# Three unused SBUF tiles that move the start addresses of two operand rings in a two-layer decoder trunk

## The chip, the cores and the metric

The kernel runs on one core of one Trainium2 chip. The metric is the device time of one execution in microseconds, the median of the runs shown; lower is better. Engines are named as the profile names them: PE (TensorE's matmuls), PEld (TensorE's weight loads), DVE (VectorE), ACT (ScalarE), POOL (GpSimd), SP (the queue that issues all DMAs here).

## What is computed

Two layers over 256 tokens of 1,024 channels, all in float32. Cut to the parts that matter here:

```python
def hybrid_layer(x, ...):
    h = rms_norm(x, g_mix)
    z = h @ w_in                       # 1024 -> 6072 columns
    ...                                # z is split among three mixers and their gates
    o_a = mla_mixer(...); o_b = conv_mixer(...); o_c = nsa_mixer(...)
    x = x + (g_a * o_a + g_b * o_b + g_c * o_c) @ w_out
    h = rms_norm(x, g_ffn)
    x = x + jnp.square(jax.nn.relu(h @ w_ff1)) @ w_ff2    # 1024 -> 4096 -> 1024
    return x
```

## The kernel before

**Every large product is three products.** A float32 operand is split into a high part (`hi`, rounded to the PE's `float32r` format by ACT, line 153 for weights) and a low part (`lo`, the remainder, by DVE, line 154). PE then adds up high by high, high by low and low by high. Weights are streamed from DRAM in pieces of 128 x 1,024 numbers by `raw` (line 138, a ring of five buffers) and split by `piece` into one of two rings: ring one is four `hi` and four `lo` buffers of the pool `wp`; ring two is the tag `big` of the pool `ap`, five buffers of 8 KB, where a tile holds two pieces side by side (`hi2`, `lo2`).

**Which operand is stationary.** In `gemm_b` (lines 163 to 165) the weight slice, 128 x 128, is the stationary operand, which a weight load brings into the array, and the activations, 256 tokens wide, are the moving one. So run the products into `psB` (the input projection's columns for convolution, low ranks and gates), the three mixer projections `wo` of 256 columns, and the first feed-forward product `ff1` (the profile cuts the name to `ff`). In `gemm_a` (lines 171 to 173) it is the other way round: 128 tokens of the activations are stationary and up to 512 weight columns move. So run `psA` (three groups of the input projection), the output projection (also called `wo` in the profile, at lines 171 to 173), and the second feed-forward product into `f0` to `f3` (`f` in the profile), whose stationary tiles are `rh` and `rl`, the two parts of the squared ReLU (lines 890 and 892).

**Activation rings.** The tag `hh` of the pool `ap` holds two buffers for the high parts, `hl` two for the low parts. Their tenants are in turn `hh`/`hl` (normed input), `oh`/`ol` (attention outputs), `mh`/`ml` (gated sum, in the first buffer), `h2`/`l2` (second norm's input). The convolution's output `yh` lies in the ring `cv` and `yl` in the ring `s2`, both of the pool `sp`. `rh` and `rl` lie in the ring `pa` of the pool `sp`, six buffers of 2 KB.

**Order.** Inside the mixer part of a layer a table (`TRACE`, with the priorities of `URGENCY`) sets the order; the framework's scheduler then places every instruction on its engine's queue. The feed-forward part is a loop over 16 groups (line 903): `ff1(gi + 1)` issues 48 matmuls of 256 columns, then `acc_pass` issues 24 matmuls of 512 columns for group `gi` (two weight pieces, two token blocks, two column halves, three products each). In the last three groups the order differs (`tail`), and there the pieces of the last group lie in ring one.

**Addresses.** Pools lie one behind the other in a partition and tags in order of first request; a tile's start is rounded up to 32 bytes. Every slice that the products below read begins a multiple of 512 bytes into its tile (only the 312-column pieces of the first `psA` group differ), so the start of the tile modulo 512 is also that of the slice. For a matmul's moving slice and stationary slice, "320 apart" means below that these two remainders differ by 320.

| tiles | first byte of the ring, before | modulo 512 | modulo 64 |
|---|---|---|---|
| `hi`, `lo` (ring one) | 54,912 / 71,296 | 128 | 0 |
| `hh`, `oh`, `mh`, `h2` | 87,680 | 128 | 0 |
| `hl`, `ol`, `ml`, `l2` | 104,064 | 128 | 0 |
| `hi2`, `lo2` (ring two, `big`) | 137,664 | 448 | 0 |
| `yl` (`s2`) | 182,912 | 128 | 0 |
| `yh`, `ca`, `upad` (`cv`), two buffers | 195,552 and 200,128 | 480 and 448 | 32 and 0 |
| `rh`, `rl`, softmax tiles `nP`, `mP`, ... (`pa`) | 209,824 | 416 | 32 |

`yh` is in the buffer at 480 in the first layer and at 448 in the second; the tap accumulator `ca` is in the other one.

Of the kernel before, what the change touches and what calls it, by code (L numbers as in the profile page):

```python
# [8 lines left out]
F32 = mybir.dt.float32  # L9
# [7 lines left out]
P = 128  # L17
# [68 lines left out]
def trunk_kernel(ctx: ExitStack, tc: tile.TileContext, A, out, depth=DEPTH):  # L86
# [4 lines left out]
    ap_ = ctx.enter_context(tc.tile_pool(name="ap", bufs=1))  # L91
    sp = ctx.enter_context(tc.tile_pool(name="sp", bufs=2))
# [5 lines left out]
    def stat(n, name, dt=F32):  # L98
        return sp.tile([P, n], dt, tag="st%d" % n, name=name, bufs=2 if n > 64 else 6)
# [36 lines left out]
    def raw(src, n):  # L136
        r = wp.tile([P, 1024], F32, tag="raw", name="raw", bufs=RB)[:, :n]
        nc.sync.dma_start(out=r, in_=src)
        return r
# [27 lines left out]
    def gemm_a(ps, ah, al, wh, wl, ks, first=True, last=True):  # L167

        n = len(ks)
        for i, (kw, ka) in enumerate(ks):  # L170
            mm(ps, lhsT=ah(ka), rhs=wh(kw), start=(first and i == 0), stop=False)  # L171
            mm(ps, lhsT=ah(ka), rhs=wl(kw), start=False, stop=False)  # L172
            mm(ps, lhsT=al(ka), rhs=wh(kw), start=False, stop=(last and i == n - 1))  # L173
# [5 lines left out]
    def rsqrt(v, p, n, name):  # L179

        s = stat(n, name + "_s", I32)
        y = stat(n, name + "_y")
        h = stat(n, name + "_h")
        t = stat(n, name + "_t")
        s, y, h, t = s[:p], y[:p], h[:p], t[:p]
        ts(out=s, in0=v.bitcast(I32), scalar1=1, scalar2=None, op0=ALU.logical_shift_right)
        ts(out=h, in0=v, scalar1=-0.5, scalar2=None, op0=ALU.mult)
        ts(out=y.bitcast(I32), in0=s, scalar1=-1, scalar2=0x5f3759df, op0=ALU.mult, op1=ALU.add)
        for _ in range(3):
            if n == 1:  # L190
                ts(out=t, in0=y, scalar1=y, scalar2=h, op0=ALU.mult, op1=ALU.mult)
                ts(out=y, in0=t, scalar1=1.5, scalar2=y, op0=ALU.add, op1=ALU.mult)
            else:
                tt(out=t, in0=y, in1=y, op=ALU.mult)
                tt(out=t, in0=t, in1=h, op=ALU.mult)
                stt(out=y, in0=t, scalar=1.5, in1=y, op0=ALU.add, op1=ALU.mult)
        return y
# [56 lines left out]
    def layer(l):  # L254
# [18 lines left out]
        def pa(name, dt=F32):  # L273
            return sp.tile([P, 512], dt, tag="pa", bufs=PA, name=name)
# [3 lines left out]
        col = lambda ap: ap.rearrange("p (n o) -> p n o", o=1)  # L278


        hh = ap_.tile([P, 8, T], R32, tag="hh", name="hh", bufs=2)
        hl = ap_.tile([P, 8, T], R32, tag="hl", name="hl", bufs=2)
        grow = raw(bass.AP(tensor=A["gmix"].tensor, offset=A["gmix"].offset + l * D, ap=[[0, P], [1, D]]), D)
        vs = stat(2, "n1v")
# [36 lines left out]
        def part_a(i):  # L321

            return ([psum(t, "psA%d" % i) for t in (("at", "at"), ("po", "ch"), ("at", "at"))[i]],
                    [piece(A["wA%d" % i][l, kp], 2, ring=int(i == 1), half=kp % 2) for kp in range(4)])

        def add_a(i, pw, b, kps=range(4)):
            for kp in kps:
                wh, wl = pw[1][kp]
                gemm_a(pw[0][b][:, :A_COLS[i]], hA(hh, b), hA(hl, b), lambda k: wh[:, k, :], lambda k: wl[:, k, :],
                       [(k, kp * 2 + k) for k in range(2)], first=(kp == 0), last=(kp == 3))  # L330
# [59 lines left out]
        def a_queries():  # L390
            nonlocal nr
            pw = part_a(2)
            psA = pw[0]
            for kp in range(4):
                for b in range(NB):
                    add_a(2, pw, b, (kp,))
            for b in range(NB):
                pq = psA[b].rearrange("p (g j d) -> p g j d", g=2, j=4)
                sq = pa("nsqq").rearrange("p (n d) -> p n d", d=DH)
                qn.append(pa("qn").rearrange("p (n d) -> p n d", d=DH))  # L400
                act(sq.rearrange("p (j g) d -> p g j d", g=2), pq, AF.Square)
                act(qn[b].rearrange("p (j g) d -> p g j d", g=2), pq, AF.Copy)
                nc.vector.tensor_reduce(out=nst[:, b, 0:8], in_=sq, axis=AX.X, op=ALU.add)
            nv = stat(24, "nv")
            ts(out=nv, in0=nst.rearrange("p b n -> p (b n)"), scalar1=1.0 / DH, scalar2=EPS, op0=ALU.mult, op1=ALU.add)
            nr = rsqrt(nv, P, 24, "nr").rearrange("p (b n) -> p b n", b=NB)
# [412 lines left out]
        def gated(m, c2):  # L819
# [13 lines left out]
            if len(done[c2]) == 3:  # L833
                if mh is None:
# [5 lines left out]
        oh = ap_.tile([P, 8, T], R32, tag="hh", name="oh", bufs=2)  # L840
        ol = ap_.tile([P, 8, T], R32, tag="hl", name="ol", bufs=2)
        steps = {"a": a_products, "a0": a_compressed, "a1": a_keys, "a2": a_queries, "qk": nsa_qk, "glu": glu, "lr": low_rank, "lrn": low_rank_norm, "ckv": compress_kv, "csc": compress_scores,
                 "nsa": lambda j: nsa_attention(j, (oh, ol)), "mla": lambda j: mla_attention(j, (oh, ol)),
                 "rk": rotary_keys, "mq": mla_q, "mk": mla_k, "tap": lambda i: taps(TAPS[i], TAPS[i + 1]), "cn": conv_norm,
# [80 lines left out]
    for l in range(depth):  # L925
        layer(l)
# [129 lines left out]
```

## Time and profile before

| | |
|---|---|
| median of 3 runs | 930.91 us (928.43, 930.91, 931.38) |
| the profiled execution's own time | 932.83 us |
| its span, first to last instruction | 930.9 us |
| granted clock, mean over the span | 0.996 of full speed |

The profiled execution took 1.92 us longer than the median of the runs and 1.9 us longer than its own span. A row of the profile gives an instruction's start and a modelled end. A matmul's listed duration holds its pipeline's latency, so the time that a matmul costs in a stream is not its duration but the distance from its start to the next start; the text below calls this the pitch, and takes it from two starts and the number of matmuls between them.

### The profile page before, as it was taken

What the parts mean: (1) busy time and instruction counts of PE and PEld (TensorE: products, weight loads), DVE (VectorE), ACT (ScalarE), POOL (GpSimd) and SP (SyncE); (2) the same over time, 40 slices, a digit from 0 to 9 for tenths busy, and PEclk for the clock granted to TensorE, in tenths of its full rate; (3) what the DMA queues carried; (4) which work ended last, traced back from release to release, by engine and by line L of the source; (5) the groups of instructions that cost most, each with busy time, mean ns of one, the idle gap of its engine ahead of it and who ended that gap; (6) DMA issues with size and microseconds to landing.
All of it is one profiled execution on the core that took longest, in us unless ns stands there. A gap on an engine that the chain in (4) does not pass through costs nothing.

```text
span 930.9 us, 16102 instructions
## 1 busy us (share of the span) xinstructions
PE 909.1 (98%) x6214; PEld 805.4 (87%) x6214; DVE 642.6 (69%) x1431; ACT 538.4 (58%) x987; POOL 27.2 (3%) x80
## 2 busy tenths in 40 slices
PE   5999999999999999999999999999999999999998
PEld 4899888689988999999878989877999789999996
DVE  6598889775787655555576989979558775555552
ACT  5456566897367644444355575679865565444430
POOL 3210000000000000000001000000000000000000
PEclk9999899999999999999999999999999999999999
DMA  8654522334565655555345553225435476555521
GB/s 292 209 166 151 203 87 80 99 126 140 182 204 194 223 194 182 190 190 186 101 158 187 162 215 106 74 80 181 159 101 194 150 259 203 185 187 186 189 91 46
DMA packets 43133, 151.55 MB, mean 163 GB/s; under 512 B 4784, under 2 KB 5680, under 8 KB 43056
## 3 DMA queue, kind: packets, MB, share of 16 engines
q1 hardware_dynamic: 43056, 150.52, 49.3%
q8 instruction: 49, 0.80, 0.3%
q14 instruction: 28, 0.23, 0.1%
HBM read 149.45 MB, written 1.05 MB: 162 GB/s over the span
## 4 chain that ended last, share of the span: by engine, by line
PE 86%; DVE 6%; DMA 4%; ACT 2%; issue 1%; SPq 0%; DVEq 0%; ACTq 0%
PE psB L163 7%; PE psB L165 7%; PE psB L164 7%; PE f L173 6%; PE f L171 6%; PE f L172 6%; PE ff L164 6%; PE ff L163 6%; PE ff L165 6%; DVE lo L154 3%; PE wo L164 2%; PE wo L163 2%; PE wo L165 2%; PE nS L576 2%; PE uq L638 2%; PE psA L172 2%
## 5 line engine op out<-in xcount | busy, mean ns | idle before, releaser
L154 DVE TENSOR_TENSOR lo<-raw,hi 128x1024 fp32r<-128x1024 f32 (+1 forms) x266 | 317.6, 1209 | 173.4 <-ACT hi L153 135.2
L153 ACT ACTIVATE hi<-raw 128x1024 fp32r<-128x1024 f32 (+1 forms) x266 | 274.7, 1048 | 262.0 <-DMA raw<-in_ff_dram 102.3
L163 PE MATMUL psB<-hh,hi 128*128 128x256 f32 x592 | 173.3, 293 | 1.4 <-ACT ug L749 1.4
L165 PE MATMUL psB<-hh,lo 128*128 128x256 f32 x592 | 171.2, 291 | 0.0
L164 PE MATMUL psB<-hl,hi 128*128 128x256 f32 x592 | 170.4, 288 | 0.0
L165 PE MATMUL ff<-h,lo 128*128 128x256 f32 x512 | 144.5, 283 | 0.0
L163 PE MATMUL ff<-h,hi 128*128 128x256 f32 x512 | 144.4, 283 | 0.0
L164 PE MATMUL ff<-l,hi 128*128 128x256 f32 x512 | 144.3, 283 | 0.0
L163 PEld LDWEIGHTS psB<-hh,hi 128*128 128x128 f32 x592 | 113.9, 192 | 8.2 <-issue 4.4
L165 PEld LDWEIGHTS psB<-hh,lo 128*128 128x128 f32 x592 | 113.7, 193 | 3.0 <-issue 2.6
L164 PEld LDWEIGHTS psB<-hl,hi 128*128 128x128 f32 x592 | 114.0, 193 | 0.3
L758 DVE SCALAR_TENSOR_TENSOR ca<-upad,cols,ca 128x256 f32<-128x256 f32 x240 | 103.6, 477 | 0.3
L173 PE MATMUL f<-hi,rl 128*128 128x512 f32 x256 | 101.2, 395 | 1.4 <-DVE rl L892 0.7
L171 PE MATMUL f<-hi,rh 128*128 128x512 f32 x256 | 101.2, 395 | 0.0
L172 PE MATMUL f<-lo,rh 128*128 128x512 f32 x256 | 101.0, 395 | 0.0
L163 PEld LDWEIGHTS ff<-h,hi 128*128 128x128 f32 x512 | 97.9, 192 | 1.2
L164 PEld LDWEIGHTS ff<-l,hi 128*128 128x128 f32 x512 | 98.0, 192 | 1.1
L165 PEld LDWEIGHTS ff<-h,lo 128*128 128x128 f32 x512 | 98.0, 192 | 0.0
L173 PEld LDWEIGHTS f<-hi,rl 128*128 128x128 f32 x256 | 48.0, 188 | 13.8 <-DVE rl L892 2.5
L171 PEld LDWEIGHTS f<-hi,rh 128*128 128x128 f32 x256 | 48.1, 188 | 10.4 <-ACT rh L890 0.2
L172 PEld LDWEIGHTS f<-lo,rh 128*128 128x128 f32 x256 | 48.0, 188 | 10.3
L172 PE MATMUL psA<-lo,hh 128*128 128x512 f32 (+1 forms) x96 | 36.0, 375 | 2.1 <-DVE lo L154 2.1
(279 smaller groups left out, 1422.5 us busy)
## 6 DMA issues: line engine op xcount, KB each, us to landing
raw<-in_ff_dram SPq DMA_DIRECT2D x128, 512.0 KB, 4.1
raw<-in_wB_dram SPq DMA_DIRECT2D x74, 512.0 KB, 3.8
raw<-in_wA_dram SPq DMA_DIRECT2D x16, 512.0 KB, 4.4
raw<-in_w_out_dram SPq DMA_DIRECT2D x16, 512.0 KB, 3.5
raw<-in_wo_nsa_dram SPq DMA_DIRECT2D x8, 512.0 KB, 4.7
raw<-in_wo_mla_dram SPq DMA_DIRECT2D x8, 512.0 KB, 4.0
raw<-in_wconv_dram SPq DMA_DIRECT2D x8, 512.0 KB, 3.9
raw<-in_wA_dram SPq DMA_DIRECT2D x8, 312.0 KB, 5.2
```

The lines of the kernel that those rows point to most:

```text
L153: act(hi, r, AF.Copy)
L154: tt(out=lo, in0=r, in1=hi.bitcast(F32), op=ALU.subtract)
L163: mm(ps, lhsT=wh(kw), rhs=ah(ka), start=(first and i == 0), stop=False)
L164: mm(ps, lhsT=wh(kw), rhs=al(ka), start=False, stop=False)
L165: mm(ps, lhsT=wl(kw), rhs=ah(ka), start=False, stop=(last and i == n - 1))
L171: mm(ps, lhsT=ah(ka), rhs=wh(kw), start=(first and i == 0), stop=False)
L172: mm(ps, lhsT=ah(ka), rhs=wl(kw), start=False, stop=False)
L173: mm(ps, lhsT=al(ka), rhs=wh(kw), start=False, stop=(last and i == n - 1))
L576: mm(pS[g].rearrange("p (h z k) -> p h z k", h=nj, z=2)[:, i], lhsT=qTn[gs, 2 * jp + j, b * P:(b + 1) * P], rhs=kTn[gs, :, 0:nk], start=Tr ...
L638: mm(ps[:, :n], lhsT=cq[:, k, b * P:(b + 1) * P], rhs=w[i][:, c0:c0 + n], start=(i == 0), stop=(i == len(ks) - 1))
L758: stt(out=ca[:, i], in0=upad[:, i, k:k + T], scalar=K("wdw", 31 * i + k), in1=ca[:, i], op0=ALU.mult, op1=ALU.add)
```

## The change

Three tiles are requested that nothing writes or reads: 80 floats (320 bytes of each partition) ahead of the ring `hh`, 48 floats (192 bytes) ahead of `hl`, and 8 floats (32 bytes) in `sp`, at the point where the ring `pa` is first requested.

```diff
@@ layer(l), line 280 on
+        if l == 0:
+            ap_.tile([P, 80], F32, tag="gap0", name="gap0")
         hh = ap_.tile([P, 8, T], R32, tag="hh", name="hh", bufs=2)
+        if l == 0:
+            ap_.tile([P, 48], F32, tag="gap1", name="gap1")
         hl = ap_.tile([P, 8, T], R32, tag="hl", name="hl", bufs=2)
@@ a_queries()
                     add_a(2, pw, b, (kp,))
+            if l == 0:
+                sp.tile([P, 8], F32, tag="gap2", name="gap2", bufs=1)
             for b in range(NB):
```

The instructions of PE, DVE, ACT, POOL and SP, their order on each engine, and what each waits for stand as before: no row of any engine differs but for line and buffer numbers. Only addresses differ. The gaps move the `hh` ring by 320 bytes, everything from `hl` to the ring ahead of `pa` by 512 bytes, and `pa` and all that follows it by 544.

| tiles | modulo 512, before | now | modulo 64, before | now |
|---|---|---|---|---|
| `hi`, `lo` (ring one) | 128 | 128 | 0 | 0 |
| `hh`, `oh`, `mh`, `h2` | 128 | 448 | 0 | 0 |
| `hl`, `ol`, `ml`, `l2` | 128 | 128 | 0 | 0 |
| `hi2`, `lo2` (ring two) | 448 | 448 | 0 | 0 |
| `yl`; `yh` | 128; 480 and 448 | 128; 480 and 448 | 0; 32 and 0 | 0; 32 and 0 |
| `rh`, `rl` and the rest of `pa` | 416 | 448 | 32 | 0 |

## Rows read from the trace of the kernel before

**Rows 1.** The page, parts 1 and 2: span, busy time, granted clock.

```profile
span 930.9 us, 16102 instructions
PE 909.1 (98%) x6214; PEld 805.4 (87%) x6214; DVE 642.6 (69%) x1431; ACT 538.4 (58%) x987; POOL 27.2 (3%) x80
PEclk9999899999999999999999999999999999999999
```

**Rows 2.** The page, part 4: the chain that ended last, by engine.

```profile
PE 86%; DVE 6%; DMA 4%; ACT 2%; issue 1%; SPq 0%; DVEq 0%; ACTq 0%
```

**Rows 3.** Busy time by stretch: one feed-forward group; one mixer stretch of layer two.

```profile
core 0: us, PE busy (x) PEld busy (x) DVE busy (x) ACT busy (x) POOL busy (x), PEclk, DMA share, GB/s
768.21:779.53 11.32, 11.32 (x74) 10.24 (x73) 5.87 (x6) 5.76 (x7) 0.00 (x0) 1.00 0.65 214
...
515.32:532.66 17.34, 17.33 (x144) 17.00 (x142) 17.14 (x31) 9.57 (x17) 0.00 (x0) 1.00 0.50 157
```

**Rows 4.** Groups of PE matmuls by line: count, busy us, mean ns.

```profile
L163 PE MATMUL psB<-hh,hi 128*128 128x256 f32 x592 | 173.3, 293 | 1.4 <-ACT ug L749 1.4
L165 PE MATMUL ff<-h,lo 128*128 128x256 f32 x512 | 144.5, 283 | 0.0
L171 PE MATMUL f<-hi,rh 128*128 128x512 f32 x256 | 101.2, 395 | 0.0
...
L163 PE MATMUL wo<-oh,hi 128*128 128x256 f32 x128 | 37.1, 290 | 0.0
...
L171 PE MATMUL wo<-hi,mh 128*128 128x512 f32 x64 | 25.2, 393 | 0.0
L171 PE MATMUL psA<-hi,hh 128*128 128x512 f32 x64 | 25.1, 392 | 1.1 <-ACT hi L153 1.1
```

**Rows 5.** Timeline of PE, one feed-forward group: start us, us, instruction.

```profile
779.53 0.39 PE L171 MATMUL f<-hi,rh 128*128 128x512 f32 x1
...
785.11 0.28 PE L163 MATMUL ff<-h,hi 128*128 128x256 f32 x1
...
790.86 0.39 PE L171 MATMUL f<-hi,rh 128*128 128x512 f32 x1
```

**Rows 6.** Timeline of PE, layer two: first and next start of two 512-column runs.

```profile
493.31 0.39 PE L171 MATMUL psA<-hi,hh 128*128 128x512 f32 x1
...
504.20 0.28 PE L163 MATMUL psB<-hh,hi 128*128 128x256 f32 x1
...
725.24 0.40 PE L171 MATMUL wo<-hi,mh 128*128 128x512 f32 x1
...
730.76 0.40 PE L171 MATMUL wo<-hi,mh 128*128 128x512 f32 x1
```

**Rows 7.** Timeline of PE, layer two: two 256-column runs and what follows them.

```profile
696.67 0.28 PE L163 MATMUL wo<-oh,hi 128*128 128x256 f32 x1
...
708.19 0.28 PE L163 MATMUL wo<-yh,hi 128*128 128x256 f32 x1
...
719.60 0.39 PE L171 MATMUL wo<-hi,mh 128*128 128x512 f32 x1
```

**Rows 8.** The second of those runs: count, duration ns min/median/max, first and last start.

```profile
L163 PE MATMUL wo<-yh,hi x32: 278/279/282, 708.2 to 719.2; 128*128 128x256 f32 x32
L164 PE MATMUL wo<-yl,hi x32: 279/285/290, 708.3 to 719.4; 128*128 128x256 f32 x32
L165 PE MATMUL wo<-yh,lo x32: 276/279/280, 708.4 to 719.5; 128*128 128x256 f32 x32
```

**Rows 9.** Groups of DVE: the convolution's taps, layer one, then layer two.

```profile
L758 DVE SCALAR_TENSOR_TENSOR ca<-upad,cols,ca 128x256 f32<-128x256 f32 x120 | 51.8, 477 | 0.2
...
L758 DVE SCALAR_TENSOR_TENSOR ca<-upad,cols,ca 128x256 f32<-128x256 f32 x120 | 51.8, 478 | 0.2
```

**Rows 10.** Groups of PE: transposes of softmax tiles, and of keys for comparison.

```profile
L555 PE MATMUL nT<-cst,nP 128*128 128x128 f32 x96 | 18.6, 278 | 0.3 <-ACT nP L550 0.3
...
L555 PE MATMUL mT<-cst,mP 128*128 128x128 f32 x48 | 8.3, 274 | 0.0
...
L677 PE MATMUL mT<-cst,xk 128*96 128x128 f32 x32 | 4.5, 275 | 0.0
```

## The prediction, made before the change was run

> **What bounds the kernel now.** I read the page's busy shares first, then the chain, then stretches, then starts in the timeline. PE is busy 98% of the span at a granted clock of nearly full speed throughout [rows 1], and the chain that ended last runs through PE for 86% of the span [rows 2]. The next question is stage by stage whether PE streams or waits. In a feed-forward group PE is busy all 11.32 us, while DVE needs 5.87, ACT 5.76 and the DMA engines a share of 0.65 of them [rows 3]: there PE alone sets the time, and each nanosecond taken off a matmul's pitch shortens the kernel. In the mixer stretch of the same view DVE is busy 17.14 of 17.34 us beside PE: there a faster PE may only wait longer for DVE.
>
> A matmul's pitch is what counts, and the trace has the same shape at different pitches. With 512 moving columns:
> - the second feed-forward product, f: 779.53 to 785.11 holds 24 matmuls [rows 5], (785.11 - 779.53) / 24 = 232.5 ns;
> - the third group of psA, weights in ring one: 48 matmuls from 493.31 to 504.20 [rows 6], 226.9 ns;
> - the output projection's second half, weights in ring two: 24 matmuls from 725.24 to 730.76 [rows 6], 230.0 ns.
>
> With 256 moving columns:
> - ff1: 48 matmuls from 785.11 to 790.86 [rows 5], 119.8 ns;
> - wo with oh and ol: 96 from 696.67 to 708.19 [rows 7], 120.0 ns;
> - wo with yh and yl: 96 from 708.19 to 719.60 [rows 7], 118.9 ns.
>
> What the runs of one width differ in is where their operands start, by the address table of the kernel before. In psA's third group both slices start at 128 modulo 512: 0 apart, 226.9 ns. In the output projection's second half they are 320 apart: 230.0. In f the stationary slice starts at 416, off the 64-byte grid, the moving one at 448: 232.5. With 256 columns, ff1 and wo with oh are 0 apart in all three products (120); with yh of layer two the high-part products are 320 apart, the low-part one 0 (118.9).
>
> **The change, part by part.** No instruction, order or wait changes, so nothing is queued anew anywhere; only pitches can.
>
> *f's stationary tiles move from 416 to 448.* They are then on the 64-byte grid and 0 apart from ring two, which is psA's third group's relation, so I take 226.9 ns. There are three lines of 256, 768 matmuls [rows 4]; 48 of them (the last group of each layer) have weights in ring one and come to be 320 apart, so 230.0 for those. 720 x (232.5 - 226.9) = 4.03 us and 48 x 2.5 = 0.12 us: **4.15 us**, all on the path. Bounds: 0 if f's pitch has another cause; nothing nearer than psA's 226.9 suggests more.
>
> *hh, h2, oh move from 128 to 448, hl, l2, ol stay at 128.* As moving operands against ring one they take exactly the remainders of yh and yl in layer two, so I take 118.9 ns. ff1 has three lines of 512, 1,536 matmuls [rows 4], x 0.9 ns = **1.4 us**, all on the path. wo with oh has 384 [rows 4] x 1.1 = **0.4 us**, streaming without a gap [rows 7]. psB has 1,776 [rows 4] x 1.1 = 1.95 us, of which I count half, **1.0 us**: its mean of 293 ns against ff1's 283 [rows 4] shows that many of them come out of a wait, and the mixer stretch has DVE busy nearly throughout. This price is the least sure. The run with yh is a mixture: its high-part lines have a median of 279 ns and a minimum of 276 against ff1's 283, its low-part line a median of 285 and a maximum of 290 [rows 8]. If every such matmul came out at 279, 4 ns less, the gain on 1,536 + 384 + 888 would be 11.2 us instead of 2.8; if the high-part ones came out at 290, 7 ns more, two thirds of 2,808 would cost 13.1 us. I take the run's mean because it is the one quantity that a whole stream showed.
>
> *As stationary operands* hh and mh go from 0 to 320 apart from ring one (psA's third group and half of the output projection, 192 matmuls by rows 4, a quarter of each) and from 320 to 0 apart from ring two (as many). At 3.1 ns (230.0 - 226.9) on two products in three each side is 0.4 us, with opposite signs: **0**.
>
> *The other tiles.* The gaps' own requests issue nothing. Softmax tiles in pa move onto the 64-byte grid too; transposes of them take 278 and 274 ns, those of xk, which starts on the grid, 275 [rows 10], so at most 144 x 3 = 0.4 us; I take 0. DVE does not see it: the tap accumulator lies 32 bytes off the grid in one layer and on it in the other, and a tap takes 477 and 478 ns [rows 9].
>
> **Sum:** 4.15 + 1.4 + 0.4 + 1.0 = 6.95 us, 7.0. The profiled execution took 932.83 us, so 925.8 by it; it stands 1.92 above the median of the runs, 930.91, and against that I predict **923.9 us**.
>
> [...]
>
> **The rivals.**
>
> *Addresses are not the cause.* f would differ from psA's third group by something else, such as spreading over four PSUM tiles or alternating between weight halves. For it: no two runs in this trace differ in the address alone. Against it: the output projection spreads over four PSUM tiles as well, and runs at 230.0. Then nothing moves: 930.9 us. A weak form, in which f only reaches 230.0 and the 256-column streams stay, gains 768 x 2.5 = 1.9 us: 929.0. Both lie within 0.3%, 2.8 us, about what a measurement of this kernel can tell from no change. I give the first 11% and the weak form 6%. [...]
>
> *The high-part streams fall into the slow step.* In ff1, psB and wo two products in three come to be 320 apart; if they settle at the slow durations that the yl line shows, up to 290 ns, and not at the run's mean, the loss sits on the path in the feed-forward part. For it: 320 apart costs 3.1 ns where the activations are stationary. Against it: the run with yh, with the same remainders, has a lower mean. At 5 ns, the middle between 3.1 and 7: 2,808 x 2/3 x 5 = 9.4 us lost, 4.15 won back in f, 5.2 us slower: 936.1 us. It decides from 4.15 / 1,872 = 2.2 ns per high-part matmul on. 10%.
>
> *All 256-column streams reach 279 ns.* Then 11.2 + 4.15 = 15.4 us go: 915.5 us. For it: two of the three lines of the run with yh have that median. Against it: its mean is not. 10%.
>
> **How the numbers follow.** The forecast keeps 63%; its own range is 920 to 926: psB's part wholly won or wholly lost is 1.0 us either way, and the 2.8 us of the 256-column streams doubled or those of ff1 and wo halved (0.9 us) make the rest. Faster by over 0.3%: 63 + 10 = 73%. Within it: 11 + 6 = 17%. Slower by more: 10%. The range leaves out the slow rival and half of the fast one: 916 to 932, the upper end the no-change case with a microsecond for the spread of its runs.
>
> **What would show it.** Right: f's 24 matmuls take 5.45 us from first start to the next product, ff1's 48 take 5.71, so that a feed-forward group takes 11.16 us instead of 11.33, with counts and waits as before and DVE's durations unchanged. f at 232 falls with the first rival; ff1 above 122 with the second; ff1 below 117 with the third. If the groups shorten as said and the end does not, the mixers have given it back to DVE's waits. The forecast is wrong if f stays above 230 or the time is outside 920 to 926.

## The result and the profile after

The changed kernel takes 925.01 us, the median of eight runs (922.98 to 926.87), against 928.72 for the kernel before in the same comparison (eight runs, 927.54 to 931.38). The two medians are 3.7 us apart. The ratio on record is 0.9944, with a 95% interval of 0.9916 to 0.9972: by it 0.56%, or 5.2 us of 930, is gained, 2.6 to 7.8 by the interval, which holds the 3.7 too. The forecast was 7.0 us (923.9).

The profiled executions are 9.6 us apart (932.83 and 923.20), and not all of that is the change's. The page of the changed kernel, parts 1, 2 and 4 (as in [rows 1, 2]):

```profile
span 921.2 us, 16102 instructions
PE 900.9 (98%) x6214; PEld 799.5 (87%) x6214; DVE 642.0 (70%) x1431; ACT 538.1 (58%) x987; POOL 28.1 (3%) x80
...
PEclk9999999999999999999999999999999999999999
...
PE 89%; DVE 5%; ACT 3%; DMA 2%; issue 1%; SPq 0%; DVEq 0%; ACTq 0%
```

PE lost 8.2 us of busy time and PEld, whose weight loads go with the matmuls, 5.9; no other engine moved by more than 1 us. But the granted clock has lost the dip that stood in [rows 1]. Busy time by stretch shows it, of the kernel before (its columns are those of [rows 3]; the last two stretches are in a mixer of layer two):

```profile
76.03:87.64 11.61, 11.61 (x96) 11.61 (x97) 11.48 (x33) 7.97 (x21) 0.00 (x0) 1.00 0.30 90
87.64:98.99 11.35, 11.35 (x59) 9.54 (x58) 6.92 (x32) 5.86 (x16) 0.00 (x0) 0.70 0.90 328
...
515.32:532.45 17.13, 17.12 (x143) 16.92 (x141) 16.93 (x30) 9.56 (x16) 0.00 (x0) 1.00 0.50 158
534.49:545.98 11.49, 11.49 (x96) 11.49 (x97) 11.37 (x33) 7.97 (x21) 0.00 (x0) 1.00 0.34 93
```

and of the changed kernel, the same work from the second on:

```profile
86.93:95.18 8.25, 8.25 (x60) 6.59 (x58) 6.23 (x27) 5.83 (x16) 0.00 (x0) 1.00 0.93 334
...
509.04:526.05 17.01, 16.98 (x142) 16.77 (x142) 16.87 (x30) 9.59 (x16) 0.00 (x0) 1.00 0.52 160
528.09:539.48 11.39, 11.39 (x96) 11.39 (x96) 11.28 (x33) 7.97 (x21) 0.00 (x0) 1.00 0.31 93
```

The stretch from 87.64 took 3.1 us longer in the profiled execution before, at a mean granted clock of 0.70: it was 0.50 from 91.0 to 97.8 us, 6.8 of the 11.35 us, and 1.00 in the rest. I count that as this execution's own: it took 932.83 us where the eight runs of the kernel before end at 931.38, and two kernels with other addresses below were profiled at a lowered clock too: `e4_both_off_grid` at a mean of 0.994, `e8_sweep_c` at 0.995, there with psB's starts 0.21 us apart between 94.6 and 97.2 us and 0.12 just after 99.6. PE's waits on other engines, added up, are another 1.6 us shorter (17.6 us before, 16.0 after). 4.9 us are left, between the 3.7 of the medians and the 5.2 of the ratio.

The rows that answer to [rows 5 to 7] are PE's timeline in layer two (start us, us, instruction): first psA's third group up to the product after it, then `wo` with `oh`, `wo` with `yh`, the output projection, and one feed-forward group.

```profile
486.73 0.39 PE L171 MATMUL psA<-hi,hh 128*128 128x512 f32 x1
...
497.92 0.28 PE L163 MATMUL psB<-hh,hi 128*128 128x256 f32 x1
...
689.71 0.28 PE L163 MATMUL wo<-oh,hi 128*128 128x256 f32 x1
...
701.12 0.28 PE L163 MATMUL wo<-yh,hi 128*128 128x256 f32 x1
...
712.54 0.39 PE L171 MATMUL wo<-hi,mh 128*128 128x512 f32 x1
...
718.18 0.39 PE L171 MATMUL wo<-hi,mh 128*128 128x512 f32 x1
...
723.72 0.39 PE L171 MATMUL wo<-hi,mh 128*128 128x512 f32 x1
...
771.78 0.39 PE L171 MATMUL f<-hi,rh 128*128 128x512 f32 x1
...
777.25 0.28 PE L163 MATMUL ff<-h,hi 128*128 128x256 f32 x1
...
782.96 0.39 PE L171 MATMUL f<-hi,rh 128*128 128x512 f32 x1
```

| stream | matmuls | pitch before | after |
|---|---|---|---|
| f | 24 in 5.47 us | 232.5 ns | 227.9 |
| ff1 | 48 in 5.71 us | 119.8 | 119.0 |
| `wo` with `oh`, `ol` | 96 in 11.41 us | 120.0 | 118.9 |
| `wo` with `yh`, `yl` | 96 in 11.42 us | 118.9 | 119.0 |
| psB, the last window above | 95 in 11.39 us | 120.9 | 119.9 |
| psA, third group | 48 in 11.19 us | 226.9 | **233.1** |
| output projection, second half | 24 in 5.54 us | 230.0 | **230.8** |

A feed-forward group takes 11.18 us instead of 11.33. The two streams whose stationary operand lies in the `hh` ring became slower. ff1 is no longer even: in the kernel before its starts are 120 ns apart, now 116 to 118, but for every second matmul of the low activations (`ff<-l,hi`, every sixth of the stream), which takes 127 to 128 ns to the next start. Groups by line show the same from the duration's side (columns as in [rows 4]: count, busy us, mean ns, idle time before):

```profile
L163 PE MATMUL psB<-hh,hi 128*128 128x256 f32 x592 | 170.6, 288 | 1.4 <-ACT ug L755 1.4
L165 PE MATMUL ff<-h,lo 128*128 128x256 f32 x512 | 142.8, 280 | 0.0
L171 PE MATMUL f<-hi,rh 128*128 128x512 f32 x256 | 100.5, 392 | 0.0
...
L764 DVE SCALAR_TENSOR_TENSOR ca<-upad,cols,ca 128x256 f32<-128x256 f32 x240 | 103.7, 479 | 0.3
```

PE's wait for `ug` is 1.4 us as in [rows 4], and a tap on DVE takes 479 ns against 478 and 477 [rows 9].

### The profile page after: what moved, and what is told of

It is laid out like the page before. It is cut to its first block, busy times and chain, and to the rows that moved or that the text cites. A ratio compares the mean times of both kernels' runs of the same rounds, so it can differ in the third digit from the quotient of the medians.

```text
span 921.2 us, 16102 instructions
## 1 busy us (share of the span) xinstructions
PE 900.9 (98%) x6214; PEld 799.5 (87%) x6214; DVE 642.0 (70%) x1431; ACT 538.1 (58%) x987; POOL 28.1 (3%) x80
## 4 chain that ended last, share of the span: by engine, by line
PE 89%; DVE 5%; ACT 3%; DMA 2%; issue 1%; SPq 0%; DVEq 0%; ACTq 0%
PE psB L163 7%; PE psB L164 7%; PE psB L165 7%; PE f L173 6%; PE f L171 6%; PE ff L164 6%; PE f L172 6%; PE ff L165 6%; PE ff L163 6%; PE wo L164 3%; PE wo L163 3%; PE wo L165 2%; PE nS L582 2%; DVE lo L154 2%; PE psA L172 2%; PE psA L173 2%
## 5 line engine op out<-in xcount | busy, mean ns | idle before, releaser
L163 PE MATMUL psB<-hh,hi 128*128 128x256 f32 x592 | 170.6, 288 | 1.4 <-ACT ug L755 1.4
L165 PE MATMUL psB<-hh,lo 128*128 128x256 f32 x592 | 168.5, 286 | 0.0
L163 PE MATMUL ff<-h,hi 128*128 128x256 f32 x512 | 142.3, 279 | 0.0
L163 PEld LDWEIGHTS psB<-hh,hi 128*128 128x128 f32 x592 | 111.4, 188 | 8.2 <-issue 4.4
L165 PEld LDWEIGHTS psB<-hh,lo 128*128 128x128 f32 x592 | 111.0, 188 | 3.0 <-issue 2.6
L164 PEld LDWEIGHTS psB<-hl,hi 128*128 128x128 f32 x592 | 111.5, 188 | 0.3
L164 PEld LDWEIGHTS ff<-l,hi 128*128 128x128 f32 x512 | 96.1, 188 | 1.1
L165 PEld LDWEIGHTS ff<-h,lo 128*128 128x128 f32 x512 | 96.0, 188 | 0.0
```

Source lines behind the costliest of these rows:

```text
L163: mm(ps, lhsT=wh(kw), rhs=ah(ka), start=(first and i == 0), stop=False)
L164: mm(ps, lhsT=wh(kw), rhs=al(ka), start=False, stop=False)
L165: mm(ps, lhsT=wl(kw), rhs=ah(ka), start=False, stop=(last and i == n - 1))
```

## The experiments

My theory: a stream's pitch depends on **d**, the start of the stationary slice minus that of the moving one, modulo 512. The rivals: it depends on whether a start lies on the 64-byte grid; or the pieces of the change act only together. In every run the instructions and their order are those of the kernel before, and only gaps differ. Diffs are against the changed kernel unless said otherwise.

**Each part alone.** `e1_gap2_only` keeps only the 32 bytes ahead of `pa`, `e2_gap01_only` only the two gaps around the `hh` ring (diffs against the kernel before).

```diff
+            if l == 0:
+                sp.tile([P, 8], F32, tag="gap2", name="gap2", bufs=1)
```

> Only the 32-byte gap ahead of the ring pa, so that rh and rl begin at 448 modulo 512 as in the change, while hh and hl stay at 128. If the start addresses of f's own operands set its pitch, f falls from 232.4 to 227.7 ns as in the change, ff1 stays at 119.8 and the third psA group at 226.9, and the time falls by 720 x 4.65 ns = 3.3 us against the kernel before. If instead the moved hh ring is what quickened f, f stays at 232.4 and the time with it.

```diff
+        if l == 0:
+            ap_.tile([P, 80], F32, tag="gap0", name="gap0")
...
+        if l == 0:
+            ap_.tile([P, 48], F32, tag="gap1", name="gap1")
```

> Only the gaps of 320 and 192 bytes, so that hh, oh, mh and h2 begin at 448 and all else where it was modulo 512. If each product answers to its own two operands, ff1, wo with oh, and psB stream at 118.9 ns, psA's third group at 233, f at 232.4; saved are 1.4 us in ff1, 0.4 in wo and up to 1.7 in psB, lost 0.6 in psA's third group and 0.6 in the rest of psA and the output projection: 2.3 us faster than before. If the 256-column gain in the change came from somewhere else, ff1 stays at 119.8 and the time is 1.2 us slower than before.

PE's timeline of a feed-forward group of the first:

```profile
421.34 0.39 PE L171 MATMUL f<-hi,rh 128*128 128x512 f32 x1
...
426.83 0.28 PE L163 MATMUL ff<-h,hi 128*128 128x256 f32 x1
...
432.58 0.39 PE L171 MATMUL f<-hi,rh 128*128 128x512 f32 x1
```

and of the second:

```profile
418.81 0.28 PE L163 MATMUL ff<-h,hi 128*128 128x256 f32 x1
...
424.51 0.39 PE L171 MATMUL f<-hi,rh 128*128 128x512 f32 x1
...
430.10 0.28 PE L163 MATMUL ff<-h,hi 128*128 128x256 f32 x1
```

With the 32 bytes alone f has 228.7 ns and ff1 the 119.8 of before; the ratio is 0.9970 (0.9954 to 0.9986), 2.8 us. With the other two alone ff1 has 118.7 and f 233, psA's third group 233.1, and the ratio is 0.9982 (0.9963 to 1.0001), 1.7 us, which by itself is not clear of zero. The product of the two ratios is 0.9952 against 0.9944 for the whole, so the parts seem to add up; the intervals are wide, and the pitches say it more plainly: each stream answered to the gap that moved its own operands.

**Grid or distance.** `e3_moving_off_grid` moves ring two by 32 bytes and leaves `pa` where it is, so that the moving slices of f start off the 64-byte grid and the stationary ones on it (d = 480 as before the change). `e4_both_off_grid` adds a `gap2` of 16 floats instead of 8: both off the grid and d = 0.

```diff
+        if l == 0:
+            ap_.tile([P, 8], F32, tag="gapb", name="gapb")
...
+                if l == 0:
+                    ap_.tile([P, 120], F32, tag="gapb2", name="gapb2")
```

> The change, with ring two (hi2, lo2, f's moving operand) moved by 32 bytes to 480, off the 64-byte grid; rh and rl stay at 448 on the grid. If it is the stationary start on the grid that made f faster, f stays at 227.7 ns. If it is the distance of 0 instead of 32 between the two starts, f goes back to about 232.4.

> The change, with ring two and the ring pa both at 480 modulo 512: f's moving and stationary starts are 0 apart, and both lie 32 bytes off the 64-byte grid. If only the distance modulo 512 counts, f runs at 227 to 228.5 ns as in the change. If the grid counts for itself, f stays at 232 to 233.

PE's timeline of a feed-forward group, moving slices alone off the grid:

```profile
421.56 0.39 PE L171 MATMUL f<-hi,rh 128*128 128x512 f32 x1
...
427.16 0.28 PE L163 MATMUL ff<-h,hi 128*128 128x256 f32 x1
```

and both off the grid:

```profile
411.95 0.39 PE L171 MATMUL f<-hi,rh 128*128 128x512 f32 x1
...
417.41 0.28 PE L163 MATMUL ff<-h,hi 128*128 128x256 f32 x1
```

f has 233.3 ns in the first and 227.5 in the second. Both slices 32 bytes off the grid cost nothing (227.5 ns against the 227.9 of the changed kernel), so the grid theory falls, and d = 480 gives nearly the same pitch with the other operand off the grid (232.5 in the kernel before). (The single times were 926.47 and 928.03; one run each ranks nothing.)

**The low parts too.** `e5_low_too` puts the 192 bytes behind the `hl` ring, so that it moves with `hh` and all three products have the same d.

```diff
-        if l == 0:
-            ap_.tile([P, 48], F32, tag="gap1", name="gap1")
         hl = ap_.tile([P, 8, T], R32, tag="hl", name="hl", bufs=2)
+        if l == 0:
+            ap_.tile([P, 48], F32, tag="gap1b", name="gap1b")
```

> The change, with hl, ol, ml and l2 moved to 448 as well, so that in ff1, wo and psB all three products are 320 apart and in the output projection and psA the two stationary rings have one remainder again. If a product's pitch is its own (117.3 ns where 320 apart, 121.9 for the low part at 0), the low line falls to 117.3 too: ff1, wo and psB stream at 117.3, which is 1.6 ns x 1,920 = 3.1 us in ff1 and wo and up to 2.5 in psB; psA's third group goes to 230 and its second to 227. Together 4 to 6 us faster than the change. If the slow step every sixth matmul is the price of two fast ones, and only the mean counts, ff1 stays near 119 to 120 and the time within 1 us of the change.

Its median is 919.05 us, ratio 0.9879 (0.9859 to 0.9900): it beats both kernels. PE's timeline, a feed-forward group and psA's third group:

```profile
406.95 0.40 PE L171 MATMUL f<-hi,rh 128*128 128x512 f32 x1
...
412.40 0.28 PE L163 MATMUL ff<-h,hi 128*128 128x256 f32 x1
...
418.05 0.40 PE L171 MATMUL f<-hi,rh 128*128 128x512 f32 x1
...
484.01 0.39 PE L171 MATMUL psA<-hi,hh 128*128 128x512 f32 x1
...
495.21 0.28 PE L163 MATMUL psB<-hh,hi 128*128 128x256 f32 x1
```

ff1 falls to 117.7 ns, and its slow sixth matmul is gone. psB's 96 matmuls of the last window above fall to 114.5 in layer two, while the same stretch of layer one has 118.9. But psA's third group has 233.3, where I had put 230: d = 320 is not d = 192 (the output projection's 230.0). With 512 columns the **sign** of the distance counts here.

**A sweep of d.** Three kernels with other gaps, and with the `hh` and `hl` buffers lengthened by 16 or 32 floats, so that the two buffers of a ring differ in d. The second of them:

```diff
-            ap_.tile([P, 80], F32, tag="gap0", name="gap0")
-        hh = ap_.tile([P, 8, T], R32, tag="hh", name="hh", bufs=2)
+            ap_.tile([P, 96], F32, tag="gap0", name="gap0")
+        hh = ap_.tile([P, 2064], R32, tag="hh", name="hh", bufs=2)[:, :8 * T].rearrange("p (k t) -> p k t", t=T)
...
-                sp.tile([P, 8], F32, tag="gap2", name="gap2", bufs=1)
+                sp.tile([P, 40], F32, tag="gap2", name="gap2", bufs=1)
```

> Stationary start minus moving start, modulo 512, set to 384 for psB, 256 for ff1 and wo, 64 for f, 128 for psA's third group, 320 for its second; high and low rings alike. If the pitch is a function of that difference and of the width alone, psA's second group runs at 233 (the third group's pitch at 320), psB and ff1 each at one steady pitch between 116 and 121, and f at 64 at the pitch that psA's second group has at 64 in the next run. If only being equal or not matters, all 512-column runs here lie at 230 to 233 and all 256-column ones at 117.7.

> The same difference set to 128 for psB, 64 for ff1 and wo, 128 for f, 384 for psA's third group, 64 for its second. By the function of the difference, f at 128 has the pitch that psA's third group has at 128 in the run before, and psA's second group at 64 that of f in the run before, within 1 ns. If the product and not the difference sets the pitch, these pairs differ by more.

> The same difference set to 448 for psB, 320 for ff1 and wo, 256 for f and for psA's second group, 64 for its third. By the function of the difference, f and psA's second group agree within 1 ns here, and psA's third group at 64 agrees with f of the first sweep; ff1 lies between 116 and 121. If the sign does not matter, ff1 at 320 has the 117.7 ns that it had at 192; psA's 233.2 at 320 against 229.9 at 192 says that it does.

PE's timeline of a feed-forward group of `e7_sweep_b` (d = 128 in f, 64 in ff1):

```profile
413.57 0.28 PE L163 MATMUL ff<-h,hi 128*128 128x256 f32 x1
...
419.02 0.39 PE L171 MATMUL f<-hi,rh 128*128 128x512 f32 x1
...
424.60 0.28 PE L163 MATMUL ff<-h,hi 128*128 128x256 f32 x1
```

ff1 takes 113.5 ns here and f 232.5. The same of `e8_sweep_c` (d = 256 in f, 320 in ff1):

```profile
410.39 0.39 PE L171 MATMUL f<-hi,rh 128*128 128x512 f32 x1
...
415.82 0.28 PE L163 MATMUL ff<-h,hi 128*128 128x256 f32 x1
...
421.48 0.39 PE L171 MATMUL f<-hi,rh 128*128 128x512 f32 x1
```

By starts to the nanosecond (the lines are rounded) f takes 226.6 ns, among its values at 0, and ff1 117.8, as it did at 192 in `e5_low_too`: with 256 columns the sign makes no difference here. Over all streams whose three products have one d, but for the output projection at 0, the values fall on one table, with d modulo 256 (for psB they are means of whole windows, which begin with some 24 slower matmuls):

| d modulo 256 | 512 columns, ns | 256 columns, ns |
|---|---|---|
| 0 | 226.6 to 228.7 (f, psA; also at d = 256) | 119.5 to 120.0 |
| 32 | | 118.3 |
| 64 | 233.0 to 233.5 (f, psA; also at d = 320) | 113.3 to 115.4, or 117.7 to 118.9 |
| 96 | 234.4 (psA) | 118.5 to 119.8 |
| 128 | 231.7 to 233.3 (f, psA) | 119.5 to 119.8 |
| 160 | 233.2 (psA) | |
| 192 | 228.9 to 230.0 (psA, output projection) | 114.3 to 115.4, or 117.7 to 118.9 |
| 224 | 232.5 to 233.3 (f) | |

With 512 columns f and psA agree within about 2 ns at the same d, so between them it is not the product that matters (the output projection's second half has 228.6 and 230.7 ns at 0, in the two layers of `e5_low_too`); with 256 columns different products do so but at 64 and 192. A difference of d by 256 made none for 512 columns: 226.6 ns at 256, 233.1 to 233.3 at 320. The two widths want opposite things here: 0 is best for 512 columns (226.6 to 228.7 ns) and worst for 256 (119.5 to 120.0). The single times were 929.52, 919.54 and 921.18 us.

**A version from the table.** `e9_best` puts `hh`, `hl`, ring two and `pa` all at 64: d = 64 for psB and ff1, 0 for f.

```diff
-            ap_.tile([P, 80], F32, tag="gap0", name="gap0")
+            ap_.tile([P, 112], F32, tag="gap0", name="gap0")
...
-            ap_.tile([P, 48], F32, tag="gap1", name="gap1")
...
+            ap_.tile([P, 48], F32, tag="gap1b", name="gap1b")
...
-                sp.tile([P, 8], F32, tag="gap2", name="gap2", bufs=1)
+                sp.tile([P, 40], F32, tag="gap2", name="gap2", bufs=1)
...
+                    ap_.tile([P, 96], F32, tag="gapb2", name="gapb2")
```

> Every stream at the best difference that the sweeps showed: psB, ff1 and wo at 64, f and psA's second group and the second half of the output projection at 0, with hh, hl, ring two and the ring pa all at 64 modulo 512; psA's third group and the other half come to 448. If the pitch is a function of the difference, ff1 runs at 114.2 and f at 227 to 228 ns: 1,536 x 5.6 = 8.6 us and 720 x 5 = 3.6 us saved against the kernel before, wo 384 x 4 = 1.5 us, psB 4 to 7 us, psA and the output projection about 0.3 us lost. Sum 17 to 20 us, 910 to 913 us where the kernel before takes 930. If DVE's taps hold the mixers, psB's part stays away: 913 to 915. If the sweep's pitches were those of that run's order of streams and not of the difference, ff1 stands above 117 and the time above 917.

The median is 917.87 us, ratio 0.9869 (0.9841 to 0.9897): it beats both kernels, but misses the 910 to 913 and lands in the expectation's last case, ff1 above 117 and the time above 917. Its timeline says why:

```profile
404.92 0.40 PE L171 MATMUL f<-hi,rh 128*128 128x512 f32 x1
...
410.38 0.28 PE L163 MATMUL ff<-h,hi 128*128 128x256 f32 x1
...
416.04 0.40 PE L171 MATMUL f<-hi,rh 128*128 128x512 f32 x1
```

f has 227.5, but ff1 117.9 at the d that gave 113.5 in `e7_sweep_b`. Two psB stretches of layer two in this one kernel, at d = 64 both, differ as well (busy time by stretch):

```profile
504.96:514.82 9.86, 9.86 (x85) 9.86 (x85) 9.72 (x18) 6.34 (x12) 0.00 (x0) 1.00 0.55 175
523.66:534.56 10.90, 10.90 (x96) 10.90 (x96) 10.90 (x33) 8.08 (x21) 0.00 (x0) 1.00 0.32 94
```

By their starts, 83 matmuls run at 118.8 ns in the first and 95 at 114.7 in the second. Each begins with 24 slower matmuls (121.2 and 118.8 ns); after these the pitch is 117.8 in the first and 113.3 in the second. So at d = 64 a stream of 256 columns had two steady pitches, and at 192 too: past the slower beginnings the two psB windows of layer two in `e5_low_too` run at 117.8 and 113.4 ns.

**A finer step.** `e10_sweep_32` has d = 32 in ff1 and 96 in psB (other gaps, and buffers lengthened by 16 floats as in the sweep).

> Differences off the grid for the wide products: 96 for psB, 32 for ff1 and wo, with all activation starts a multiple of 32 that for psB and for ff1 is no multiple of 64; f at 0. If the pitch follows the difference smoothly, ff1 at 32 lies between 119.8 (at 0) and 114.2 (at 64), and psB at 96 between 114 and 118.9 (at 128). If a start off the 64-byte grid costs by itself, both lie above 120.

ff1 has 118.3, psB 118.5 to 119.8, psA's second group at d = 96 234.4. The 256-column streams stay below 120, so no grid shows here either. ff1 lies in between, as I had put; of psB's two windows the one of layer one does (118.5), that of layer two (119.8) does not. Past their slower beginnings the two run at 117.4 and 118.7: a second pitch at one d shows here too, if a closer one. One run: 923.03 us.

**Which pitch of the two.** Two kernels take the two differences between `e7_sweep_b` and `e9_best` apart: `e11_mode_f128` moves `pa` alone, so that f runs at d = 128; `e12_mode_big448` leaves ring two and `pa` at 448 (diffs against `e9_best`).

```diff
-                sp.tile([P, 40], F32, tag="gap2", name="gap2", bufs=1)
+                sp.tile([P, 72], F32, tag="gap2", name="gap2", bufs=1)
```

> ff1 at a difference of 64 ran at 113.3 ns in the second sweep, where f stood at 128 (232.4 ns) and ring two at 448 modulo 512, and at 117.8 in the version put together from the sweeps, where f stood at 0 (227.8) and ring two at 64. This run has f at 128 and ring two at 64. If f's own stream sets the phase in which ff1 starts, ff1 runs at 113.3 to 114, a feed-forward group takes 48 x 113.7 + 24 x 232.4 = 11.04 us, and the time is 2 us under the put-together version's 917.9. If the place of ring two against the first ff1 weights decides, ff1 stays at 117.8, the group takes 11.23 us and the time is 921.

```diff
-            ap_.tile([P, 48], F32, tag="gap1b", name="gap1b")
+            ap_.tile([P, 16], F32, tag="gap1b", name="gap1b")
...
-                sp.tile([P, 40], F32, tag="gap2", name="gap2", bufs=1)
+                sp.tile([P, 8], F32, tag="gap2", name="gap2", bufs=1)
...
-                    ap_.tile([P, 96], F32, tag="gapb2", name="gapb2")
```

> The fourth combination: f at 0 and ring two at 448, ff1, wo and psB at 64. If the place of ring two decides, ff1 runs at 113.3 to 114 behind a fast f: a feed-forward group takes 48 x 113.7 + 24 x 227.7 = 10.92 us, 28 x 0.2 = 5.6 us under the put-together version, less 0.8 us for psA's second group and half of the output projection at 128: 913 us. If f's own stream decides, ff1 stays at 117.8 and the time is 918.7.

The timeline of `e11_mode_f128`:

```profile
412.61 0.28 PE L163 MATMUL ff<-h,hi 128*128 128x256 f32 x1
...
418.06 0.39 PE L171 MATMUL f<-hi,rh 128*128 128x512 f32 x1
...
423.62 0.28 PE L163 MATMUL ff<-h,hi 128*128 128x256 f32 x1
...
429.27 0.40 PE L171 MATMUL f<-hi,rh 128*128 128x512 f32 x1
```

and of `e12_mode_big448`:

```profile
416.02 0.28 PE L163 MATMUL ff<-h,hi 128*128 128x256 f32 x1
...
421.68 0.39 PE L171 MATMUL f<-hi,rh 128*128 128x512 f32 x1
```

With f at d = 128 and ring two at 64, ff1 has 113.5 ns in one group and 117.8 in the next (5.45 us and 5.65). With f at 0 and ring two at 448 it has 117.9 in the group shown, with f at 0 and ring two at 64 (`e9_best`) likewise, and with f at 128 and ring two at 448 (`e7_sweep_b`) 113.5 in the group shown, after 117.7 in an early one from 303.1 us on. `e12_mode_big448` came out as its second case had it, by which f's own stream decides (918.95 us); `e11_mode_f128` came out between its two cases (919.18 us). So the stream's own d does not decide alone: in these groups f's d and ring two's place both made a difference. Whether the work ahead of the stream is what counts was not shown, and what picks the pitch stays open. The ratios, 0.9878 (0.9854 to 0.9902) and 0.9881 (0.9855 to 0.9906), overlap with those of `e5_low_too` and `e9_best`: the four can't be ranked.

## Why the prediction was right, point by point

- **The bound.** Right: PE is busy 98%, no wait took the gain away, and a shorter pitch in a feed-forward group shortened the group by as much. The fear that the mixers would give it back to DVE did not come true: the 140 psB matmuls of the stretch of [rows 3] took 17.01 us instead of 17.13 with DVE busy 16.87 of them.
- **f, 4.15 us.** Right in cause, too large: a steady group gains 4.6 ns a matmul, not 5.6, and all 768 together, with the last groups and without waits, 3.1 us; f alone (`e1_gap2_only`) brought 2.8 us. It landed at 227.9, not 226.9. Half of the reason was wrong: f was slow by its distance of 480 (233.3 at that distance in `e3_moving_off_grid` too), and the 64-byte grid played no part (both off it, 227.5).
- **ff1, 1.4 us and `wo`, 0.4 us.** (119.8 - 119.0) x 1,536 = 1.3 us, and 1.1 x 384 = 0.4: as forecast.
- **psB, 1.0 us.** Too small: 0.9 to 1.0 ns where it streams and 1.5 us in all, waits left out, because the matmuls that ran beside a busy DVE gained too.
- **hh and mh as stationary operands, 0.** This step failed, in "from 0 to 320 apart [...] and from 320 to 0 apart [...] each side is 0.4 us, with opposite signs". "320 apart" dropped the sign. Before, ring two stood at d = 128 - 448 = 192 (modulo 512), which costs 230; now ring one stands at 448 - 128 = 320, the same as 64, which costs 233. And the other side won nothing back: the output projection's second half has 230.8 after 230.0, and the last 18 matmuls of psA's second group, whose weights lie in ring two as well, 231.3 after 228.9. They begin here before the change, and end at the 493.31 of [rows 6],

```profile
489.19 0.39 PE L171 MATMUL psA<-hi,hh 128*128 128x512 f32 x1
```

and here after it, and end at 486.73:

```profile
482.57 0.39 PE L171 MATMUL psA<-hi,hh 128*128 128x512 f32 x1
```

There the high parts came to 0 while the low parts kept 192; with the low parts at 0 too (`e5_low_too`) these 18 run at 227.2 and the output projection's second half at 228.6 (in layer one 230.7). So the mixture of distances won nothing; why it does not come out as the mean of its parts stays open. psA's third group loses 6.2 ns x 48 = 0.3 us in a layer; all of psA loses 1.1 us in two layers, 0.6 of it in the third groups, and the output projection 0.1, waits left out.

The sum is then 3.1 + 1.4 + 0.4 + 1.5 - 1.2 = 5.2 us, each term taken over the two profiles matmul by matmul, against 5.2 by the ratio and 3.7 by the medians. The forecast's 7.0 was the right mechanism, with f a quarter too large and a loss of 1.2 us in the term put at 0. That 925.0 us lies so near the 923.9 is in part luck: the forecast counted from 930.9, and the kernel before had 928.7 in the comparison. From 930.9 the same gain would have ended at 925.7 to 927.2, and the range ended at 926.

The rivals: that addresses are not the cause falls by the two parts alone and by the sweep. The slow step came, but not as the rival had it: every sixth matmul takes 127 to 128 ns, it is one of low activations and not of the high ones, and the faster others outweigh it, so that ff1's steady groups of 48 and the `wo` runs of 96 stand at 118.9 to 119.0 ns here, and above 120.0 in no run. The fast rival, all at 279 ns, was not this change but exists: moved with `hl` as well, these streams reach 117.7, and 113.3 at their best.

What is measured is that the same shape takes 226.6 to 234.4 ns with 512 columns and 113.3 to 120.0 with 256, in kernels with the same instructions in the same order, by where their tiles lie alone. Why the pitch goes with the distance of the two starts was not shown.

## What to carry to other kernels

Where PE bounds a kernel and one matmul shape shows different pitches, write down the start addresses of both operands and their signed difference modulo 256 bytes, before looking for waits. Gaps of some tens to hundreds of bytes were worth 0.4 to 0.6% here as changed and 1.2 to 1.3% when all rings were placed. A ring that serves as moving operand in one product and as stationary in another has two differences of opposite sign, and both, and the low parts with the high, have to be priced.

## What was not expected of the hardware

- In these runs the pitch of a float32 stream went with the distance of its operands' starts, modulo 256, by up to 7.8 ns of 230 (226.6 to 234.4) and 6.7 of 120 (113.3 to 120.0). With 512 columns the sign counted (233 ns at 64, 229 to 230 at 192), with 256 it showed no effect (ff1 at 117.7 ns at 192 and 117.8 at 320). Two starts both 32 bytes off the 64-byte grid cost nothing (227.5 ns).
- At a distance of 64 or 192 a 256-column stream had two steady pitches (about 113.5 and 118 ns). After some 24 slower matmuls, psB kept 117.8 in one stretch of `e9_best` and 113.3 in another; in `e11_mode_f128` two groups of ff1 in a row had 113.5 and 117.8.
- In the profiled execution of the kernel before, the granted clock was 0.70 over one stretch of 11.35 us (0.50 for 6.8 us of it, 1.00 in the rest), right after PE had been busy for all of 11.61 us at a clock of 1.00; in the changed kernel the same work found a clock of 1.00 throughout, after 11.51 us of a busy PE.
